# Gate and up blocks of a float32 decoder trunk: the closing adds and the silu issued later or as a side job, and the first block of a layer mixing single up chunks with its seven-product pairs

## The chip, the core and the metric

The kernel runs on one core of a Trainium2 chip. The metric is the device time of one execution in microseconds (us). TensorE is called PE here, VectorE DVE, ScalarE ACT, GpSimd POOL and the queue that issues the weight DMAs SP. All engines work their own instruction stream in order and wait for each other through semaphores.

## The reference

Two decoder layers on 256 tokens of width 2048. Each layer has a mixing part (attention, a linear recurrence and gated linear attention that share one input and one output projection) and a dense SwiGLU part. The change concerns the second:

```python
h = rms_norm(x, pre_ffn_norm[l])
hid = jax.nn.silu(einsum('bsd,df->bsf', h, w_ffn_gate[l])) * einsum('bsd,df->bsf', h, w_ffn_up[l])
ff = einsum('bsf,fd->bsd', hid, w_ffn_down[l])
x = x + rms_norm(ff, post_ffn_norm[l])
```

D is 2048 and the hidden width F is 5632. Everything is float32.

## The kernel before

**Matrix products.** Every float32 operand is split in two parts, hi (rounded to the fast matmul type) and lo (the rest), and one product is three matmuls: hi·hi, hi·lo, lo·hi (`multiply`, L393). The activations are split once. Each 128x512 chunk of weights is an *item* that must be split just before it is used: ACT copies it to hi, DVE subtracts to get lo (`split`, L301). The parts live in a ring of `NHI = 10` buffers called `hilo`, so that item n can be split only when the matmuls of item n-10 have read their buffer. Raw weights come in pieces of two chunks (512 KB) into a ring of `NRAW = 5` buffers; a piece is loaded when a slot is free (`load`, L279).

**Gate and up.** The hidden width is cut into 11 blocks of 512 (`f`), for two halves of the tokens (t = 0, 1). A block has eight pairs of chunks (`PAIRS = "CCCSCSCS"`). A C pair is done in the classic way: four items, each multiplied for both token halves (two products an item). An S pair is done with seven products in place of eight, in the manner of Strassen; its seven items are four sums of chunks made on DVE (t1 to t4) and three raw chunks. The products of an S pair are p1, p6, p7, q4, p2, q3, q5 in this order (`seven`, L435). p2, q4, q3 and x are four accumulators of the pool `acc`, used by C pairs as well; p1 sits in the PSUM tile `tr`, q5 in `o`, p6 and p7 are the two halves of the tile `sc`. So a block is 20 raw items with 40 products and 21 items with one product each: 61 products, 183 matmuls.

**The end of a block.** At the last S pair, after each product, `evac` (L1274) combines the sums: m1 is a copy of p1 (ACT); u2 = m1 + p6, u3 = u2 + p7, c21 = u3 + q4, c11 = m1 + p2, c12 = q3 - u2, c22 = x - u3 (DVE); silu of c21 and c11 (ACT); c12 and c22 get q5 added; each is scaled and multiplied with its silu (two scalar_tensor_tensor on DVE). In the profile u2 and u3 are named `u_u`, the four others `c_c`, m1 `m`. A side job, `hidden` (L1310), then transposes the result on PE into `tr` (t = 0) and `o` (t = 1), from where ACT and DVE write the split activations `uh` and `ul`. The next block's p1 and q5 use `tr` and `o` again, and `seven` demands that the job has been issued before it issues p1 (`lane.require`).

**What sets the order.** All is issued from one Python program that writes each engine's stream in the order of its calls. `feed(upto, used)` (L330) writes splits ahead: `LOOK_W = 12` items, as far as the ring lets it. At the last S pair of a block it is held back: after the seven products it may reach 0, 0, 1, 1, 2, 3 and 4 items past the block's end, and elsewhere in the block not past the end at all. Side jobs are run by `lane.tick()` when a modelled clock says that they are ready.

**The first block of a layer** (f = 0) multiplies the five classic pairs chunk by chunk: first ten gate chunks while the normalised input is still arriving, then `make_forms` (L1248, the sums of activations that the S pairs need: on DVE one add of 128x1536, four of 128x384, and three splits that ACT and DVE share), then ten up chunks, then three S pairs in a row.

After each part of four, four and three blocks come four `down` blocks over the finished hidden activations.

Of the kernel before, what the change touches and what calls it, by code (L numbers as in the profile page):

```python
# [15 lines left out]
AF = mybir.ActivationFunctionType  # L16
# [26 lines left out]


PAIRS = "CCCSCSCS"
FIRST_PAIRS = "CCCCCSSS"
N_C = PAIRS.count("C")
N_S = PAIRS.count("S")

# [1 line left out]
def pair_order(f):  # L51


    if f == 0:
        order = [(m, k) for m in range(2) for k in range(2 * N_C)]
        return order + [e for p in range(N_C, DC // 2) for e in quad(p)]
    order, at = [], {"C": 0, "S": N_C}
    for kind in PAIRS:
        p = at[kind]
        at[kind] += 1  # L60
        order += quad(p) if kind == "S" else [(m, k) for m in range(2) for k in (2 * p, 2 * p + 1)]
    return order
# [115 lines left out]
def tile_hybrid_trunk(ctx, tc, x, xT, w_in, w_out, w_gu, w_down, post_norms, lams,  # L178
# [74 lines left out]
    for l in range(DEPTH):  # L253
        for n0, n in IN_ORDER:
            plain(w_in[l][:, n0:n0 + n], DC)
        cols = [slice(b * 512, (b + 1) * 512) for b in range(4)]
        for c in cols:
            plain(w_out[l][:, c], DC)
        for f0, f1 in FFN_PARTS:
            for f in range(f0, f1):  # L260
                recipes = []
                for kind in FIRST_PAIRS if f == 0 else PAIRS:
                    i = sum(1 if r[0] == "raw" else 4 if r[0] == "b11" else 0 for r in recipes)
                    recipes += [("raw", i + j) for j in range(4)] if kind == "C" else [(name, i) for name in QUAD]
                add_block([w_gu[l, f, i] for i in range(DC)], recipes)
            for c in cols:
                plain(w_down[l][f0 * 512:f1 * 512, c], 4 * (f1 - f0))
# [3 lines left out]
    for b, (n, count) in enumerate(blocks):  # L271
        b %= per_layer
        w = b in (0, 14, 15, 16, per_layer - 2, per_layer - 1) and len(wider) > 0
        wider += [w and i % 8 in (1, 4, 6) and (b != 16 or i < 2 * N_C) for i in range(count)]
    raws, parts_of, rings = [], [], {False: [], True: []}
    before_load, before_split = {}, {}
    sums = {}
# [23 lines left out]
    def split():  # L301
        j = len(parts_of)
        b, kind, i = items[j]
        n = blocks[b][0]

        quad_of = {"b11": 1, "b21": 2, "b22": 3}
        r = raw_chunk(i + quad_of.get(kind, 0)) if kind == "raw" or kind in quad_of else sums[kind]
        before_split.pop(j, lambda: None)()
        if kind == "b11":
            up1, gate1, up2 = raw_chunk(i), raw_chunk(i + 1), raw_chunk(i + 3)  # L310
            dve.free = max(dve.free, raws[i // 2 + 1][1])
# [12 lines left out]
        dve.free = max(dve.free, act.free)  # L324
        dve.tensor_tensor(out=lo, in0=r, in1=hi.bitcast(F32), op=ALU.subtract)
        parts_of.append((hi, lo, dve.free))
        if (kind == "raw" and i % 2 or kind in ("t2", "b22")) and len(raws) < len(pieces):
            load()

    def feed(upto, used=math.inf):  # L330
# [71 lines left out]
    def pair_block(f, ah, al, forms, hidden_before, evac):  # L402
# [32 lines left out]
        def seven(j, p, final):  # L435
            if "p1" not in acc:
                lane.require(*hidden_before)
                acc["p1"] = pp.tile([P, 512], F32, tag="tr", name="gu_p1", bufs=1)
                acc["q5"] = pp.tile([P, 512], F32, tag="o", name="gu_q5", bufs=1)
                sc = pp.tile([P, 2, 512], F32, tag="sc", name="gu_p67", bufs=1)  # L440
                acc["p6"], acc["p7"] = sc[:, 0, :], sc[:, 1, :]
            s = [(forms[p][:, i, 0, :], forms[p][:, i, 1, :]) for i in range(4)]
            c = 2 * (N_C + p)
            a = {"p1": parted(c, 0), "p2": parted(c + 1, 0), "q4": parted(c + 1, 1),
                 "q5": s[0], "p6": s[1], "p7": s[2], "q3": s[3]}
            for i, k in enumerate(("p1", "p6", "p7", "q4", "p2", "q3", "q5")):
                feed(j + i + 1, used[0])
                multiply(acc[k], a[k], j + i, begin(k), final)
                used[0] = j + i + 1
                if final:  # L450
                    evac(k, acc)
                    feed(base + count + (0, 0, 1, 1, 2, 3, 4)[i], used[0])
                else:
                    feed(min(used[0] + LOOK_W, base + count), used[0])
                lane.tick()

        j = base
        if f == 0:
            at = [0, 0]
            while min(at) < 2 * N_C:  # L460
                able = [t for t in range(NT) if at[t] < 2 * N_C and (t == 1 or at[0] - at[1] < AHEAD)
                        and done.get(("h", t, at[t]), math.inf) <= lane.clk]
                if not able:
                    lane.idle()
                    continue
                t = min(able, key=lambda t: at[t])
                feed(j + at[t] + 1)
                classic(j + at[t], 0, at[t], t)
                at[t] += 1
                used[0] = j + min(at)  # L470
                if ("h", 1, 7) not in done:
                    feed(j + at[0] + LOOK_F, used[0])
                else:
                    feed(used[0] + LOOK_W, used[0])
            j += 2 * N_C
            forms.extend(make_forms(ah, al))
            for c in range(2 * N_C):
                feed(j + 1)
                for t in range(NT):
                    classic(j, 1, c, t)  # L480
                j += 1
                used[0] = j
                feed(min(j + LOOK_W, base + count), j)
            for p in range(N_S):
                seven(j, p, p == N_S - 1)
                j += 7
            return
        at = {"C": 0, "S": 0}
        for kind in PAIRS:
# [6 lines left out]
            for m in range(2):  # L496
                for c in (2 * p, 2 * p + 1):
                    feed(j + 1)
                    for t in range(NT):
                        classic(j, m, c, t)  # L500
                    j += 1
                    used[0] = j
                    feed(min(j + LOOK_W, base + count), j)


    def rsqrt(y, ss, n, inv, pre=None):
# [210 lines left out]
    for l in range(DEPTH):  # L717
# [551 lines left out]
        for part, (f0, f1) in enumerate(FFN_PARTS):  # L1269
            uh, ul = parts("uh"), parts("ul")  # L1270
            for f in range(f0, f1):
                got = {}

                def evac(k, acc, got=got, f=f, uh=uh, ul=ul):  # L1274
# [4 lines left out]
                    if k == "p1":  # L1279
# [3 lines left out]
                            pair = pm.tile([P, 2, 512], F32, tag="s4", name="_".join(names), bufs=NS4)  # L1283
                            got[names[0]], got[names[1]] = pair[:, 0, :], pair[:, 1, :]
                        act.copy(got["m1"], acc["p1"])
                    if k == "p6":
                        dve.free = max(dve.free, act.free)
                        add("u2", got["m1"], acc["p6"])
                    if k == "p7":
                        add("u3", got["u2"], acc["p7"])  # L1290
                        lane.free["sc"] = dve.free + W_DROP
                    if k == "q4":
# [3 lines left out]
                    if k == "q3":  # L1296
                        add("c12", acc["q3"], got["u2"], ALU.subtract)
                        add("c22", acc["x"], got["u3"], ALU.subtract)
                        for t, c in ((1, "c21"), (0, "c11")):
                            act.activation(got[c], got[c], AF.Silu, scale=s2f[t])  # L1300
                    if k == "q5":
                        for t, g, u in ((0, "c11", "c12"), (1, "c21", "c22")):
                            add(u, got[u], acc["q5"])
                        for t, g, u in ((0, "c11", "c12"), (1, "c21", "c22")):
                            dve.scalar_tensor_tensor(out=got[g], in0=got[u], scalar=s2f[t], in1=got[g],
                                                     op0=ALU.mult, op1=ALU.mult)
                        lane.free["tr"] = lane.free["o"] = dve.free + W_DROP
                        lane.add(0, hidden(f - f0, f, [got["c11"], got["c21"]], uh, ul))

                def hidden(c4, f, sg, uh, ul):  # L1310
                    for t in range(NT):
                        tag = "tr" if t == 0 else "o"
                        yield dve.through(0.25, tag) if t == 0 else (0.0, tag, None)
                        tp = turned(sg[t], tag, name="tpu")
                        split_scaled(uh[:, 4 * c4:4 * c4 + 4, t * P:(t + 1) * P],
                                     ul[:, 4 * c4:4 * c4 + 4, t * P:(t + 1) * P], tp, None)
                        dve.drops(tag)
# [30 lines left out]
W_SM = 0.25  # L1348
W_DROP = 0.3
W_AT = 0.1  # L1350


# [52 lines left out]
```

## Time and profile before

| what | us |
|---|---|
| median of 3 runs | 2290.61 (2290.44 to 2293.33) |
| the profiled execution, its own time | 2290.65 |
| its span, first to last instruction | 2288.8 |

| engine | busy us | share | instructions |
|---|---|---|---|
| PE weight loads | 1798.1 | 79% | 10206 |
| DVE | 1729.3 | 76% | 3175 |
| ACT | 1277.6 | 56% | 2561 |
| POOL | 13.3 | 1% | 33 |

The mean granted PE clock is 0.996. The weight DMAs move 409.75 MB in 512 KB pieces. Matmuls are pipelined: one is shown as 0.39 us long, but the next starts about 0.23 us after it. Time lost on PE is therefore best read from start to start, and idle time between the shown ends is somewhat less than what is lost. In the views a row has its start, its duration, engine, line, operation, output <- inputs, and in brackets the engine's idle time ahead of it with what ended it.

### The profile page before, as it was taken

Reading aid. Unit: us, or ns where it says so; the run is one execution under the profiler, and the core shown is the slowest. Engines: PE = TensorE matmul, PEld = TensorE weight load, DVE = VectorE, ACT = ScalarE, POOL = GpSimd, SP = SyncE. Lnnn points to the kernel's source line nnn. Section 1 sums busy time; section 2 is a strip of 40 time slices with the busy share of each in tenths; the row PEclk is TensorE's granted clock in tenths of the full one; section 3 lists DMA queues with packets and bytes.
Section 4 is the critical chain, followed back from the end, with each engine's and each line's share of the span. In section 5 each row is a group of like instructions: output and inputs, shape, how many; then the busy total and the mean of one; then the engine's idle time right before and its main releaser. Section 6 shows DMA issues by size and latency. Waiting matters only on the chain.

```text
span 2288.8 us, 30371 instructions
## 1 busy us (share of the span) xinstructions
PE 2217.9 (97%) x10206; PEld 1798.1 (79%) x10206; DVE 1729.3 (76%) x3175; ACT 1277.6 (56%) x2561; POOL 13.3 (1%) x33
## 2 busy tenths in 40 slices
PE   8999999899999999999999999998999999999998
PEld 7777878677787778877877788786777877788776
DVE  6766866898768886689786677569996588956885
ACT  6455755655545554455564467566555455544553
POOL 0000000000000000000000000000000000000000
PEclk9999999999999999999999999999999999999999
DMA  8553655365555546555654536544655555565464
GB/s 292 165 166 94 218 172 192 122 203 196 201 189 183 188 163 229 184 167 199 236 156 148 158 107 211 180 166 154 196 193 199 180 192 174 184 220 183 160 223 142
DMA packets 175068, 416.93 MB, mean 182 GB/s; under 512 B 13344, under 2 KB 24128, under 8 KB 174912
## 3 DMA queue, kind: packets, MB, share of 16 engines
q1 hardware_dynamic: 173056, 409.75, 54.3%
q0 software_dynamic: 1280, 4.20, 0.8%
q8 instruction: 80, 1.31, 0.2%
q10 hardware_dynamic: 576, 1.05, 0.1%
q14 instruction: 76, 0.62, 0.1%
HBM read 412.85 MB, written 2.10 MB: 181 GB/s over the span
## 4 chain that ended last, share of the span: by engine, by line
PE 85%; DVE 10%; issue 3%; ACT 1%; DMA 1%; SPq 0%; DVEq 0%; ACTq 0%
PE down L363 7%; PE in L362 7%; PE down L364 7%; PE down L362 6%; PE in L364 6%; PE in L363 6%; PE gu_q L398 5%; PE gu_q L399 5%; PE gu_q L397 5%; PE gu_p L397 4%; PE gu_p L399 4%; PE gu_p L398 4%; DVE hilo L158 4%; DVE c_c L158 3%; PE op L362 3%
## 5 line engine op out<-in xcount | busy, mean ns | idle before, releaser
L158 DVE TENSOR_TENSOR hilo<-raw,hilo 128x512 fp32r<-128x512 f32 (+1 forms) x1502 | 965.6, 675 | 343.9 <-ACT hilo L158 341.4
L158 ACT CAST hilo<-raw 128x512 fp32r<-128x512 f32 (+1 forms) x1502 | 857.7, 612 | 369.9 <-DVE hilo L158 183.6
L362 PE MATMUL in<-hilo,hh 128*128 128x512 f32 (+1 forms) x768 | 300.8, 392 | 6.1 <-ACT hilo L158 6.1
L364 PE MATMUL in<-hilo,hl 128*128 128x512 f32 (+1 forms) x768 | 287.4, 374 | 0.8 <-DVE hl L158 0.8
L363 PE MATMUL in<-hilo,hh 128*128 128x512 f32 (+1 forms) x768 | 286.7, 373 | 0.6 <-DVE hilo L158 0.6
L363 PE MATMUL down<-hilo,uh 128*128 128x512 f32 x704 | 274.5, 390 | 6.3 <-DVE hilo L158 6.3
L362 PE MATMUL down<-hilo,uh 128*128 128x512 f32 x704 | 274.6, 390 | 0.0
L364 PE MATMUL down<-hilo,ul 128*128 128x512 f32 x704 | 274.0, 389 | 0.0
L158 ACT CAST hilo<-t 128x512 fp32r<-128x512 f32 x264 | 162.4, 620 | 178.3 <-DVE t L158 141.9
L398 PE MATMUL gu_q<-hilo,hh 128*128 128x512 f32 x506 | 199.2, 394 | 15.4 <-DVE hilo L158 15.3
L397 PE MATMUL gu_q<-hilo,hh 128*128 128x512 f32 x506 | 197.9, 391 | 0.0
L399 PE MATMUL gu_q<-hilo,hl 128*128 128x512 f32 x506 | 197.7, 391 | 0.1
L158 DVE TENSOR_TENSOR hilo<-t,hilo 128x512 fp32r<-128x512 f32 x264 | 170.4, 684 | 4.4 <-ACT hilo L158 4.4
L362 PEld LDWEIGHTS in<-hilo,hh 128*128 128x128 f32 x768 | 145.2, 189 | 31.0 <-ACT hilo L158 6.5
L364 PEld LDWEIGHTS in<-hilo,hl 128*128 128x128 f32 x768 | 144.5, 188 | 27.5 <-DVE hl L158 1.3
L363 PEld LDWEIGHTS in<-hilo,hh 128*128 128x128 f32 x768 | 145.2, 189 | 22.4 <-DVE hilo L158 2.0
L363 PEld LDWEIGHTS down<-hilo,uh 128*128 128x128 f32 x704 | 132.2, 188 | 35.9 <-DVE hilo L158 8.8
L364 PEld LDWEIGHTS down<-hilo,ul 128*128 128x128 f32 x704 | 132.1, 188 | 27.3
L362 PEld LDWEIGHTS down<-hilo,uh 128*128 128x128 f32 x704 | 132.1, 188 | 27.1
L398 PE MATMUL gu_p<-hilo,hh 128*128 128x512 f32 x352 | 137.7, 391 | 2.3 <-DVE hilo L158 2.3
L397 PE MATMUL gu_p<-hilo,hh 128*128 128x512 f32 x352 | 137.8, 391 | 0.0
L399 PE MATMUL gu_p<-hilo,hl 128*128 128x512 f32 x352 | 137.3, 390 | 0.0
(221 smaller groups left out, 3116.0 us busy)
## 6 DMA issues: line engine op xcount, KB each, us to landing
raw<-in_w_gu_dram SPq DMA_DIRECT2D x352, 512.0 KB, 3.8
raw<-in_w_down_dram SPq DMA_DIRECT2D x176, 512.0 KB, 4.3
raw<-in_w_in_dram SPq DMA_DIRECT2D x159, 512.0 KB, 4.3
raw<-in_w_out_dram SPq DMA_DIRECT2D x64, 512.0 KB, 4.8
raw<-in_w_in_dram SPq DMA_DIRECT2D x32, 264.0 KB, 2.9
gain<-in_post_norms_dram POOLq DMA_DIRECT2D x16, 256.0 KB, 4.1
x<-in_x_dram SPq DMA_DIRECT2D x8, 256.0 KB, 7.5
xt<-in_xT_dram SPq DMA_DIRECT2D x7, 256.0 KB, 7.4
```

The lines of the kernel that those rows point to most:

```text
L158: return getattr(self.engine, name)(*args, **kwargs)
L362: nc.tensor.matmul(acc[t], ah[:, c, sl], hi, start=(i == 0), stop=False)
L363: nc.tensor.matmul(acc[t], ah[:, c, sl], lo, start=False, stop=False)
L364: nc.tensor.matmul(acc[t], al[:, c, sl], hi, start=False, stop=(i == last))
L397: nc.tensor.matmul(acc, a[0], hi, start=start, stop=False)
L398: nc.tensor.matmul(acc, a[0], lo, start=False, stop=False)
L399: nc.tensor.matmul(acc, a[1], hi, start=False, stop=stop)
```

## The change

It has four parts.

- **Order of the first block.** After the ten gate chunks the ten up chunks (U) and three S pairs are mixed: `UUUUUSUUUSUUS`. The weights are packed on the host in that order. A quad of an S pair can now lie across three pieces, so the loads follow a table, `read_by`, of pieces read to the end.
- **Look-ahead.** The limits at a block's end are gone: `feed` runs `LOOK_W` items ahead of the product just issued, across the end of the block, and at the last S pair before `evac` in place of after it.
- **u2 later.** u2 is issued after p7, with u3, in place of after p6.
- **Side job.** The two silu, the adds of q5, and the two scalar_tensor_tensor are steps of `hidden`, each at least `W_HID = 1` modelled us after the last, so that other work is written between them.

```diff
-FIRST_PAIRS = "CCCCCSSS"
+FIRST_ORDER = "UUUUUSUUUSUUS"
...
+    read_by, left = [], Counter()
+    for b, kind, i in items:
+        for c in {"raw": (i,), "b11": (i + 1,), "t2": (i,), "b21": (i + 2,), "b22": (i + 3,)}.get(kind, ()):
+            left[c // 2] += 1
+    full_at = 0
...
+        while full_at in left and left[full_at] == 0:
+            full_at += 1
+        read_by.append(full_at)
...
-        if (kind == "raw" and i % 2 or kind in ("t2", "b22")) and len(raws) < len(pieces):
+        while len(raws) < min(len(pieces), read_by[j] + NRAW):
             load()
...
                 multiply(acc[k], a[k], j + i, begin(k), final)
                 used[0] = j + i + 1
+                feed(used[0] + LOOK_W, used[0])
                 if final:
                     evac(k, acc)
-                    feed(base + count + (0, 0, 1, 1, 2, 3, 4)[i], used[0])
-                else:
-                    feed(min(used[0] + LOOK_W, base + count), used[0])
                 lane.tick()
...
             forms.extend(make_forms(ah, al))
-            for c in range(2 * N_C):
+            at = {"U": 0, "S": 0}
+            for kind in FIRST_ORDER:
+                p = at[kind]
+                at[kind] += 1
+                if kind == "S":
+                    seven(j, p, p == N_S - 1)
+                    j += 7
+                    continue
                 feed(j + 1)
                 for t in range(NT):
-                    classic(j, 1, c, t)
+                    classic(j, 1, p, t)
                 j += 1
                 used[0] = j
-                feed(min(j + LOOK_W, base + count), j)
-            for p in range(N_S):
-                seven(j, p, p == N_S - 1)
-                j += 7
+                feed(j + LOOK_W, j)
             return
...
-                    feed(min(j + LOOK_W, base + count), j)
+                    feed(j + LOOK_W, j)
...
-                    if k == "p6":
+                    if k == "p7":
                         dve.free = max(dve.free, act.free)
                         add("u2", got["m1"], acc["p6"])
-                    if k == "p7":
                         add("u3", got["u2"], acc["p7"])
                         lane.free["sc"] = dve.free + W_DROP
...
-                        for t, c in ((1, "c21"), (0, "c11")):
-                            act.activation(got[c], got[c], AF.Silu, scale=s2f[t])
                     if k == "q5":
-                        for t, g, u in ((0, "c11", "c12"), (1, "c21", "c22")):
-                            add(u, got[u], acc["q5"])
-                        for t, g, u in ((0, "c11", "c12"), (1, "c21", "c22")):
-                            dve.scalar_tensor_tensor(out=got[g], in0=got[u], scalar=s2f[t], in1=got[g],
...
+                        lane.add(0, hidden(f - f0, f, got, acc["q5"], uh, ul))
+
+                def hidden(c4, f, got, q5, uh, ul):
+                    names = ("c11", "c12"), ("c21", "c22")
+                    yield after(W_HID)
+                    for t, (g, u) in enumerate(names):
+                        act.activation(got[g], got[g], AF.Silu, scale=s2f[t])
+                        dve.tensor_tensor(out=got[u], in0=got[u], in1=q5, op=ALU.add)
+                        yield after(W_HID)
+                    lane.free["tr"] = lane.free["o"] = dve.free + W_DROP
+                    for t, (g, u) in enumerate(names):
+                        dve.free = max(dve.free, act.free)
+                        dve.scalar_tensor_tensor(out=got[g], in0=got[u], scalar=s2f[t], in1=got[g],
+                                                 op0=ALU.mult, op1=ALU.mult)
+                        yield after(W_HID)
                     for t in range(NT):
...
-                        tp = turned(sg[t], tag, name="tpu")
+                        tp = turned(got[names[t][0]], tag, name="tpu")
...
+W_HID = 1.0
```

The changed kernel has the same instructions on every engine, kind by kind; only their order differs. Three places show how.

**DVE at the end of block 1** (layer 0; the same at the end of every gate and up block). `hilo<-raw` are subtractions for the next block's first items. Before:

```order
L158 TENSOR_TENSOR hilo<-t_4650,hilo 128x512
L158 TENSOR_TENSOR u_u_4726<-m_4725,gu_p_4544 128x512
L158 TENSOR_TENSOR u_u_4726<-u_u_4726,gu_p_4544 128x512
L158 TENSOR_TENSOR hilo<-raw,hilo 128x512
L158 TENSOR_TENSOR c_c_4727<-u_u_4726,gu_q_4377 128x512
L158 TENSOR_TENSOR c_c_4727<-m_4725,gu_p_4376 128x512
```

Now:

```order
L162 TENSOR_TENSOR hilo<-t_4650,hilo 128x512
L162 TENSOR_TENSOR hilo<-raw,hilo 128x512 x6
L162 TENSOR_TENSOR u_u_4742<-m_4741,gu_p_4544 128x512
L162 TENSOR_TENSOR u_u_4742<-u_u_4742,gu_p_4544 128x512
L162 TENSOR_TENSOR hilo<-raw,hilo 128x512
L162 TENSOR_TENSOR c_c_4743<-u_u_4742,gu_q_4395 128x512
L162 TENSOR_TENSOR hilo<-raw,hilo 128x512
L162 TENSOR_TENSOR c_c_4743<-m_4741,gu_p_4394 128x512
```

Ahead of c21 (the first `c_c`) stand seven subtractions of the next block where one stood, ahead of c11 (the second) eight.

**PE around the transposes `tpu` of block 0's result** (layer 0), which lie inside block 1. Before, they stand in that block's fourth item, 51 matmuls ahead of its first p1:

```order
L399 MATMUL gu_q_4378<-hilo,hl 128x512
L551 MATMUL tpu<-ident,c_c_4327 128x128 x8
L397 MATMUL gu_x<-hilo,hh 128x512
L398 MATMUL gu_x<-hilo,hh 128x512
L399 MATMUL gu_x<-hilo,hl 128x512
L397 MATMUL gu_p_4376<-hilo,hh 128x512
```

Now they stand behind all twelve items of the first three C pairs. The first row behind them is p1 (`gu_p_4542`), which goes into the PSUM tile that the transposes of t = 0 have just filled:

```order
L417 MATMUL gu_x<-hilo,hl 128x512
L571 MATMUL tpu<-ident,c_c_4343 128x128 x8
L415 MATMUL gu_p_4542<-hilo,hh 128x512
L416 MATMUL gu_p_4542<-hilo,hh 128x512
L417 MATMUL gu_p_4542<-hilo,hl 128x512
L415 MATMUL gu_p_4544<-hilo,form 128x512
```

The job's steps take their distance, and the demand at p1 issues the rest of it at once. Counted in matmuls between the transposes and p1, this place reads 0 for blocks 0, 1 and 2, 9 for block 4, 6 for block 5, 3 for block 6, 9 for block 8 and 6 for block 9, in both layers. Behind blocks 3, 7 and 10 come `down` blocks, with no p1 near.

**DVE in the first block around `make_forms`** (the rows `mw` and `form`; layer 0). `hl` is the last of the normalised input. Before:

```order
L158 TENSOR_TENSOR hilo<-raw,hilo 128x512 x2
L158 SCALAR_TENSOR_TENSOR hl<-tpx,vec,hh 128x128 x4
L158 TENSOR_TENSOR hilo<-raw,hilo 128x512 x4
L158 TENSOR_TENSOR mw<-hh,hl 128x1536
L158 TENSOR_TENSOR mw<-mw 128x3x128 x4
L158 TENSOR_TENSOR form<-mw,form 128x4x128 x3
```

Now:

```order
L162 TENSOR_TENSOR hilo<-raw,hilo 128x512
L162 TENSOR_TENSOR t_4016<-raw 128x512
L162 TENSOR_TENSOR t_4018<-t_4016,raw 128x512
L162 TENSOR_TENSOR hilo<-raw,hilo 128x512
L162 SCALAR_TENSOR_TENSOR hl<-tpx,vec,hh 128x128 x4
L162 TENSOR_TENSOR t_4043<-raw 128x512
L162 TENSOR_TENSOR t_4045<-t_4018,raw 128x512
L162 TENSOR_TENSOR hilo<-t_4018,hilo 128x512
L162 TENSOR_TENSOR hilo<-t_4043,hilo 128x512
L162 TENSOR_TENSOR hilo<-t_4045,hilo 128x512
L162 TENSOR_TENSOR hilo<-raw,hilo 128x512
L162 TENSOR_TENSOR mw<-hh,hl 128x1536
```

The first S pair's sums and five of its splits have come ahead of `make_forms`, in place of five up chunks' splits; the first product that needs a form stood behind ten up chunks and now stands behind five.

More of the change, by code (lines that the diff above doesn't have):

```diff
@@ L54, in pair_order @@
     if f == 0:
-        order = [(m, k) for m in range(2) for k in range(2 * N_C)]
-        return order + [e for p in range(N_C, DC // 2) for e in quad(p)]
+        order, at = [(0, k) for k in range(2 * N_C)], {"U": 0, "S": N_C}
+        for kind in FIRST_ORDER:
+            order += quad(at[kind]) if kind == "S" else [(1, at[kind])]
+            at[kind] += 1
+        return order
     order, at = [], {"C": 0, "S": N_C}
@@ L261, in tile_hybrid_trunk @@
                 recipes = []
-                for kind in FIRST_PAIRS if f == 0 else PAIRS:
-                    i = sum(1 if r[0] == "raw" else 4 if r[0] == "b11" else 0 for r in recipes)
-                    recipes += [("raw", i + j) for j in range(4)] if kind == "C" else [(name, i) for name in QUAD]
+                i = 0
+                for kind in "G" * 2 * N_C + FIRST_ORDER if f == 0 else PAIRS:
+                    k = 1 if kind in "GU" else 4
+                    recipes += [(name, i) for name in QUAD] if kind == "S" else [("raw", i + j) for j in range(k)]
+                    i += k
                 add_block([w_gu[l, f, i] for i in range(DC)], recipes)
@@ L274, in tile_hybrid_trunk @@
         wider += [w and i % 8 in (1, 4, 6) and (b != 16 or i < 2 * N_C) for i in range(count)]
+    read_by, left = [], Counter()
[3 more added lines that the diff above has]
+    full_at = 0
+    for b, kind, i in items:
+        for c in {"raw": (i,), "b11": (i + 1,), "t2": (i,), "b21": (i + 2,), "b22": (i + 3,)}.get(kind, ()):
+            left[c // 2] -= 1
+        while full_at in left and left[full_at] == 0:
+            full_at += 1
+        read_by.append(full_at)
     raws, parts_of, rings = [], [], {False: [], True: []}
@@ L310, in split @@
             up1, gate1, up2 = raw_chunk(i), raw_chunk(i + 1), raw_chunk(i + 3)
-            dve.free = max(dve.free, raws[i // 2 + 1][1])
+            dve.free = max(dve.free, raws[(i + 3) // 2][1])
             summed("t1", gate1, up1, "e")
@@ L476, in pair_block @@
             forms.extend(make_forms(ah, al))
-            for c in range(2 * N_C):
+            at = {"U": 0, "S": 0}
+            for kind in FIRST_ORDER:
+                p = at[kind]
+                at[kind] += 1
+                if kind == "S":
+                    seven(j, p, p == N_S - 1)
+                    j += 7
+                    continue
                 feed(j + 1)
                 for t in range(NT):
-                    classic(j, 1, c, t)
+                    classic(j, 1, p, t)
                 j += 1
                 used[0] = j
-                feed(min(j + LOOK_W, base + count), j)
-            for p in range(N_S):
-                seven(j, p, p == N_S - 1)
-                j += 7
+                feed(j + LOOK_W, j)
             return
@@ L1298, in evac @@
                         add("c22", acc["x"], got["u3"], ALU.subtract)
-                        for t, c in ((1, "c21"), (0, "c11")):
-                            act.activation(got[c], got[c], AF.Silu, scale=s2f[t])
                     if k == "q5":
-                        for t, g, u in ((0, "c11", "c12"), (1, "c21", "c22")):
-                            add(u, got[u], acc["q5"])
-                        for t, g, u in ((0, "c11", "c12"), (1, "c21", "c22")):
-                            dve.scalar_tensor_tensor(out=got[g], in0=got[u], scalar=s2f[t], in1=got[g],
[L1306 to L1310, printed above, removed]
+                        lane.add(0, hidden(f - f0, f, got, acc["q5"], uh, ul))
[12 more added lines that the diff above has]
+                        yield after(W_HID)
                     for t in range(NT):
```

## The prediction

> **What bounds the kernel now.** The page comes first: PE is busy nearly all the time, so only PE's gaps can be won. The list of waits (who waited for whom: us in total, times, longest) says which of them lie in the gate and up blocks.
>
> ```profile
> PE 2217.9 (97%) x10206; PEld 1798.1 (79%) x10206; DVE 1729.3 (76%) x3175; ACT 1277.6 (56%) x2561; POOL 13.3 (1%) x33
> ```
> ```profile
> PE gu_p L397 <- DVE u_u L158: 22.8, 22, 2.9
> PE gu_q L398 <- DVE hilo L158: 15.3, 15, 1.1
> PE gu_p L398 <- DVE hilo L158: 9.0, 10, 1.7
> PE down L363 <- DVE hilo L158: 6.3, 6, 1.1
> ```
>
> Together 53.4 us: most of what PE stands idle. The 22 waits for `u_u` are one per block, the 21 of the second and fourth row come behind a block's end, and the ten of the third belong to the two first blocks. The timeline of PE shows the first two kinds in one block (block 2, layer 0), from p1 of its last S pair on:
>
> ```profile
> 534.51 0.39 PE L397 MATMUL gu_p<-hilo,hh 128*128 128x512 f32 x1
> ...
> 535.19 0.39 PE L397 MATMUL gu_p<-hilo,form 128*128 128x512 f32 x1
> ...
> 535.64 0.39 PE L399 MATMUL gu_p<-hilo,form 128*128 128x512 f32 x1
> 536.88 0.50 PE L397 MATMUL gu_p<-hilo,form 128*128 128x512 f32 x1 [0.85 <-DVE u_u L158]
> 537.22 0.40 PE L398 MATMUL gu_p<-hilo,form 128*128 128x512 f32 x1
> ...
> 540.44 0.39 PE L397 MATMUL gu_p<-hilo,hh 128*128 128x512 f32 x1
> ...
> 544.52 0.39 PE L397 MATMUL gu_q<-hilo,hh 128*128 128x512 f32 x1
> 545.95 0.50 PE L398 MATMUL gu_q<-hilo,hh 128*128 128x512 f32 x1 [1.04 <-DVE hilo L158]
> ...
> 546.52 1.03 PE L551 MATMUL tpu<-ident,c_c 128*128 128x128 f32 x8
> 547.31 0.47 PE L397 MATMUL gu_x<-hilo,hh 128*128 128x512 f32 x1
> ```
>
> A product takes 0.68 (534.51 to 535.19), its three matmuls 0.227 each. p7 starts at 536.88, 1.24 behind the matmul before it: 1.01 lost, and 0.11 in the step after it (0.34). At 545.95 it is 1.43: 1.20 lost, and 0.11 again. So **a block's end costs 2.43 us**; the next block starts at 540.44. DVE and ACT there:
>
> ```profile
> 538.49 0.69 DVE L158 TENSOR_TENSOR hilo<-raw,hilo 128x512 fp32r<-128x512 f32 x1
> 539.09 0.68 DVE L158 TENSOR_TENSOR c_c<-u_u,gu_q 128x512 f32<-128x512 f32 x1
> 539.69 0.68 DVE L158 TENSOR_TENSOR c_c<-m,gu_p 128x512 f32<-128x512 f32 x1
> ```
> ```profile
> 535.39 0.59 ACT L158 COPY m<-gu_p 128x512 f32<-128x512 f32 x1 [3.37 <-PE gu_p L399]
> 535.87 1.14 ACT L158 CAST hilo<-raw 128x512 fp32r<-128x512 f32 x2
> ```
>
> DVE starts an operation every 0.60 (538.49, 539.09, 539.69), ACT one every 0.5, each in the order written. c21 and c11 (the two `c_c`) end at 539.77 and 540.37, just before 540.44. That matters, because the next block's first two accumulators are the buffers that c21 and c11 have read: q4's buffer, free first, is given out first, p2's second.
>
> **The end of a block after the change.** The wait for u2 and the wait for the fourth item's split both go: u2 and u3 follow p7, and ten splits are written ahead. What is late next is c21 and c11, now behind seven and eight subtractions of the next block (41 is its first item). I walk the queues with p1's start as 0. A product has left its buffers some 0.9 after its start (m's copy of p1 starts at 535.39, p1 at 534.51), so the ring buffer of product i (0 for p1) is free at 0.68 i + 0.90. Item 44 takes p1's buffer: cast 0.90 to 1.5. Then ACT copies m1, casts item 45 at 1.9, and item 46, which needs p7's buffer (2.26), at 2.45 to 3.05. DVE subtracts 44 at 1.55, 45 at 2.6, 46 at 3.2; u2 starts at 3.8; u3, which reads it, at 4.5; a subtraction at 5.1; **c21 from 5.7 to 6.4**; a subtraction at 6.3; **c11 from 6.9 to 7.6**. PE ends the seven products at 4.76 and gets its first buffer at 6.4; three matmuls later, at about 7.2, it needs the second and gets it at 7.65, where 5.44 was due. With 0.11 for starting again 2.3 us are lost in place of 2.43. **Twenty ends (blocks 1 to 10, both layers): -2.6 us**, out of the 48.6 that were there. The adds of q5, the silu and the two last multiplications come behind these and release nothing that PE wants soon; put back ahead of c11 each would cost 0.60 on DVE.
>
> The loads don't reach this path: the last piece that the walk uses is asked for when its ring slot's last subtraction ends, about 1.8 ahead of p1, is cast at 4.3, and lands in 3.8 (first row below).
>
> ```profile
> raw<-in_w_gu_dram SPq DMA_DIRECT2D x352, 512.0 KB, 3.8
> L158 ACT CAST uh<-tpu x44: 576/586/594, 460.1 to 2222.2; 128x512 fp32r<-128x512 f32 x44
> L158 DVE TENSOR_TENSOR ul<-tpu,uh x44: 677/682/686, 463.5 to 2223.4; 128x512 fp32r<-128x512 f32 x44
> ```
>
> **A new wait: p1 behind the transposes.** Where p1 follows the transposes directly, it waits until ACT (0.59) and DVE (0.68) have read `tr`, and all of PE is queued behind it. Before shows no such wait. Bounds: nothing, if both ran beneath the eight transposes (0.79, 546.52 to 547.31); about 2 us, if both began only when all eight are done, with one cast ahead of them. Walked with the transposes' start as 0: the product before them starts at -0.68, its ring buffer is cast from 0.22 to 0.84, `uh` runs from 0.75 to 1.35; DVE subtracts that item at 0.88 and makes `ul` from 1.48 to 2.16; p1 starts at 2.2, due at 0.79. With the restart 1.5 us; I take it, nearer the upper end, since the ring puts that cast and subtraction ahead. Six places: 9 us. With three matmuls between (block 6) 0.68 more is hidden and one cast less stands ahead: 0.6, twice. With six or nine there is no wait. **Together +10.2 us.**
>
> **The first block.** DVE sets the pace here, and its work is the same in a new order.
>
> ```profile
> 421.29 1.90 DVE L158 TENSOR_TENSOR form<-mw,form 128x512 fp32r<-128x512 f32 x3 [0.69 <-ACT form L158]
> 423.10 0.15 DVE L158 TENSOR_REDUCE ss<-ssx 128x2 f32<-128x8 f32 x1
> ...
> 449.94 0.69 DVE L158 TENSOR_TENSOR c_c<-m,gu_p 128x512 f32<-128x512 f32 x1
> ```
> ```profile
> 446.26 0.79 PE L397 MATMUL gu_p<-hilo,form 128*128 128x512 f32 x1 [2.87 <-DVE u_u L158]
> ...
> 451.12 0.39 PE L397 MATMUL gu_p<-hilo,hh 128*128 128x512 f32 x1
> 456.20 0.50 PE L398 MATMUL gu_q<-hilo,hh 128*128 128x512 f32 x1 [0.62 <-DVE hilo L158]
> ```
>
> Before, block 1 starts at 451.12 and loses 0.9 at 456.20 (0.62 idle, the rest as above): as if it started at 452.0. After, six operations stand between the last `hl` and `make_forms` where four stood, two of them sums that casts wait for: the forms start 0 to 3.6 later (six operations at 0.60), I take 2.05, so at 423.35. From there to c11's end the new order has the three forms (1.8), 13 small operations of the norm (0.15 each, 2.2 with their gaps), and 41 operations of 0.60 with 0.4 for sums that read the one before: 29.0, so c11 ends at 452.4, and block 1 starts as if at 451.9. **Nothing won**: what PE no longer waits inside the block it waits at its end, 5 us in one piece. Such a piece makes the clock slow:
>
> ```profile
> 442.28:445.69 3.41, 0.73 (x2) 0.30 (x2) 3.41 (x7) 3.41 (x7) 0.00 (x0) 1.00 0.46 154
> 445.69:449.10 3.41, 2.84 (x7) 2.26 (x8) 1.67 (x3) 1.40 (x2) 0.00 (x0) 0.50 0.47 154
> ...
> 1148.84:1152.25 3.41, 2.12 (x11) 1.45 (x12) 3.41 (x9) 2.83 (x11) 0.00 (x0) 1.00 0.14 25
> ```
>
> (stretch, length, busy us of PE, PEld, DVE, ACT and POOL, granted clock, DMA). A stretch of 3.41 us with 0.73 of PE work was followed by one at 0.50, one with 2.12 was not. Before paid such a stretch already, inside the wait of 446.26; after pays it behind the block's start, up to 1.7 each. **+2 us for both layers** (0 to 3.4).
>
> **Sum**, against the profiled execution's own time: 2290.65 - 2.6 + 10.2 + 2 = 2300.3 us; its 1.85 outside the span stay. It lies within 0.1 us of the median of the runs (2290.61).
>
> **Rivals.**
> - *The clock falls at ordinary ends too.* After the change PE idles 1.5 and 0.25 (between shown ends) within 2.7 us: a stretch that holds it all has 1.65 of work, between the 0.73 that slowed and the 2.12 that did not. If half of the 22 ends fall on the bad side, 11 x 1.6 = +17.6: 2318. The Trainium skill, "TensorE: Matmul & The Clock Gate", Part 1, says that the clock halves after at least one idle window of about 3.4 us; by that no ordinary end would slow and the time would be 2300. The trace speaks against taking it to the letter: 0.73 us of work stood in the stretch ahead of 445.69.
> - *p1's wait is hidden* since ACT and DVE reach the transposed tile at once: 2290.65 - 2.6 + 2 = 2290, the same. It needs `ul` done 0.8 after the transposes' start; 0.59 and 0.68 in a row alone are more.
> - *Faster: the ends really close.* If c21 starts by 4.0 and c11 by 4.65 behind p1, PE finds both buffers free, and the ends lose nothing: 2290.65 - 48.6 + 10.2 + 2 = 2254. It needs all six subtractions done when u2 can start at 2.3, so the casts of items 44 to 46 before p1, p6 and p7 release their buffers: against the ring. For it: ACT stood idle 3.37 ahead of m.
> - *The first blocks gain* what PE lost inside them (9.0 and 2 x 2.87 of idle time, some 18 with restarts), if DVE's order frees c11 sooner: 2282. That the mixing brings nothing there is part of my forecast.
>
> **How the numbers follow.** Forecast 0.62 (its own range 2293 to 2308); slower clock 0.15; p1's wait hidden 0.13; ends close 0.06; first blocks gain 0.04. The range 2286 to 2318 leaves out the two faster cases and half of the slow-clock case. 0.2%, or 4.6 us, is what a measurement of this kernel can tell from no change: faster has the two faster cases and a sliver, 0.11; within it lie most of the hidden-p1 case and the forecast's low end, 0.18; slower keeps 0.71.
>
> **What would show it.** In the list of waits PE's waits for `u_u` are gone, as are those for `hilo` at block starts; in their place stand waits for `c_c`, two at each of 22 block ends, near 1.5 and 0.25, and eight waits of p1 for `ul`, six near 1.2. On DVE's timeline c21 starts 5.7 behind p1. The stretch from one block's last p7 to the next one's, 44.9 now, is 46.3 where p1 follows the transposes directly and 44.7 elsewhere. I am wrong if c21 starts before 4.5, if p1 waits under 0.7, or if the clock row shows 0.50 behind most ends.

## The result, and the profile after

| | median us | runs | profiled execution | its span | mean granted PE clock |
|---|---|---|---|---|---|
| before | 2290.57 | 2290.44 to 2293.33 | 2290.65 | 2288.8 | 0.996 |
| after | 2315.87 | 2312.89 to 2316.99 | 2312.89 | 2310.8 | 0.989 |

The changed kernel is slower: the ratio is 1.0106, 95% interval 1.0088 to 1.0123. The profiled execution was the fastest of its four, 3 us below their median. All sums below are made against it.

The first line of the page, with the engines' busy time, has the same counts as before. PE was busy 2217.9 before:

```profile
PE 2233.3 (97%) x10206; PEld 1809.9 (78%) x10206; DVE 1743.9 (75%) x3175; ACT 1303.8 (56%) x2561; POOL 13.3 (1%) x33
```

The same 10206 matmuls are shown busy 15.4 us longer. That is the first sign of a slower clock, since a busy time does not contain waits. The list of waits on PE (who waited for whom: us in total, times, longest):

```profile
PE gu_p L415 <- DVE c_c L162: 32.7, 16, 5.1
PE down L380 <- DVE c_c L162: 10.8, 12, 1.6
PE gu_p L415 <- DVE ul L162: 7.8, 8, 1.2
PE gu_p L415 <- ACT form L162: 6.3, 2, 3.2
...
PE gu_q L415 <- DVE c_c L162: 2.4, 14, 0.2
...
PE down L380 <- ACT uh L162: 0.8, 2, 0.4
```

The waits for `u_u` and, at block starts, for `hilo` are gone. In their place every block end waits for c21 and c11 (`c_c`), eight p1 wait for `ul`, and each first block waits once for a form. PE's timeline at the end of block 2 (layer 0), the place that the prediction showed of before; p1 of the last S pair starts at 538.53:

```profile
538.53 0.39 PE L415 MATMUL gu_p<-hilo,hh 128*128 128x512 f32 x1
...
543.06 0.39 PE L417 MATMUL gu_q<-hilo,form 128*128 128x512 f32 x1
545.08 0.47 PE L415 MATMUL gu_p<-hilo,hh 128*128 128x512 f32 x1 [1.63 <-DVE c_c L162]
545.39 0.40 PE L416 MATMUL gu_p<-hilo,hh 128*128 128x512 f32 x1
545.63 0.39 PE L417 MATMUL gu_p<-hilo,hl 128*128 128x512 f32 x1
546.19 0.50 PE L415 MATMUL gu_q<-hilo,hh 128*128 128x512 f32 x1 [0.17 <-DVE c_c L162]
546.53 0.40 PE L416 MATMUL gu_q<-hilo,hh 128*128 128x512 f32 x1
```

The four starts behind 543.06, 545.08, 545.63 and 546.19 come 2.02, 0.31, 0.56 and 0.34 later where 0.227 is normal: 2.32 lost (the second step stands between 545.08 and 545.39). The seven products themselves run without a gap. DVE there:

```profile
541.73 0.69 DVE L162 TENSOR_TENSOR hilo<-raw,hilo 128x512 fp32r<-128x512 f32 x1
542.33 0.68 DVE L162 TENSOR_TENSOR u_u<-m,gu_p 128x512 f32<-128x512 f32 x1
543.05 0.69 DVE L162 TENSOR_TENSOR u_u<-u_u,gu_p 128x512 f32<-128x512 f32 x1
543.66 0.68 DVE L162 TENSOR_TENSOR hilo<-raw,hilo 128x512 fp32r<-128x512 f32 x1
544.26 0.68 DVE L162 TENSOR_TENSOR c_c<-u_u,gu_q 128x512 f32<-128x512 f32 x1
544.86 0.68 DVE L162 TENSOR_TENSOR hilo<-raw,hilo 128x512 fp32r<-128x512 f32 x1
545.46 0.68 DVE L162 TENSOR_TENSOR c_c<-m,gu_p 128x512 f32<-128x512 f32 x1
```

c21 starts 5.73 behind p1 and ends at 544.94; PE starts at 545.08. c11 ends at 546.14; PE takes the second buffer at 546.19.

**Where the 22 us went.** For each matmul of the gate, up and down blocks and each first matmul behind transposes I took the distance to the start before it, less 0.227, and sorted the sums by what the matmul waited for; matmuls without a wait that lie in a stretch of half clock are the last row but one.

| lost on PE, us | before | after | difference | forecast |
|---|---|---|---|---|
| ends of 20 ordinary blocks | 44.4 | 42.9 | -1.5 | -2.6 |
| the two first blocks and their ends | 17.8 | 16.6 | -1.2 | 0 |
| p1 behind the transposes | 0 | 8.4 | +8.4 | +10.2 |
| `down` behind the transposes | 0 | 1.4 | +1.4 | none |
| slow clock, both first blocks | 3.9 | 8.9 | +5.0 | +2 |
| slow clock, ordinary ends | 0 | 10.0 | +10.0 | 0 |
| the rest | 3.2 | 3.4 | +0.2 | none |
| sum | 69.3 | 91.6 | +22.3 | +9.6 |

The spans differ by 22.0, so the table is complete. The ends' row after comes to 2.13 at 19 of the 20 ends; one, at 1696.42, waited 0.28 longer. The other 0.19 of the 2.32 lies in matmuls that show no wait (545.39 and 546.53) and stands in the rest.

The slow clock is seen in the view by stretches (stretch, length, busy us of PE, PEld, DVE, ACT and POOL, granted clock, DMA share, GB/s). Two ordinary ends of the changed kernel, each with the stretch behind it:

```profile
1741.82:1745.23 3.41, 1.68 (x7) 0.77 (x5) 3.38 (x7) 1.29 (x3) 0.00 (x0) 1.00 0.80 282
1745.23:1748.65 3.42, 3.35 (x8) 2.68 (x9) 3.42 (x7) 1.97 (x3) 0.00 (x0) 0.50 0.48 160
588.12:591.53 3.41, 1.78 (x9) 1.19 (x8) 3.38 (x6) 2.14 (x4) 0.00 (x0) 1.00 0.73 226
591.53:594.95 3.42, 3.25 (x14) 2.33 (x14) 3.42 (x7) 2.03 (x4) 0.00 (x0) 1.00 0.71 253
```

At the first, 1.68 us of PE work in a stretch of 3.41 were followed by a stretch at 0.50; at the second 1.78 were not. Both hold the whole long piece of 1.63 (it ends at 1744.19 and at 591.34); the first has 0.1 of the short piece as well. So between these two it is the sum of idle time in the stretch that differs, not the longest piece. The stretches lie on a grid of their own (the slow ones that begin at 724.66, 861.19 and 994.31 are 40 and 39 times 3.413 apart), so the ends of different blocks are cut by it in different places. Six of the 20 ordinary ends were slowed, at 1.60 to 1.71 us each: the 10.0 us of the table.

### The profile page after: what moved, and what is told of

The parts are those of the page before. It is cut to its first block, busy times and chain, and to the rows that moved or that the text cites. A ratio compares the mean times of both kernels' runs of the same rounds, so it can differ in the third digit from the quotient of the medians.

```text
span 2310.8 us, 30317 instructions
## 1 busy us (share of the span) xinstructions
PE 2233.3 (97%) x10206; PEld 1809.9 (78%) x10206; DVE 1743.9 (75%) x3175; ACT 1303.8 (56%) x2561; POOL 13.3 (1%) x33
## 4 chain that ended last, share of the span: by engine, by line
PE 85%; DVE 8%; issue 2%; ACT 2%; DMA 1%; SPq 0%; ACTq 0%; DVEq 0%
PE down L380 7%; PE down L382 7%; PE down L381 7%; PE in L380 6%; PE in L382 6%; PE in L381 6%; PE gu_q L415 5%; PE gu_q L417 5%; PE gu_q L416 5%; DVE hilo L162 4%; PE gu_p L415 4%; PE gu_p L416 4%; PE gu_p L417 4%; PE op L380 3%; PE op L382 3%; PE op L381 3%
## 5 line engine op out<-in xcount | busy, mean ns | idle before, releaser
L162 DVE TENSOR_TENSOR hilo<-raw,hilo 128x512 fp32r<-128x512 f32 (+1 forms) x1502 | 984.2, 676 | 420.9 <-ACT hilo L162 415.1
L162 ACT CAST hilo<-raw 128x512 fp32r<-128x512 f32 (+1 forms) x1502 | 877.8, 613 | 438.1 <-DVE hilo L162 166.3
L415 PE MATMUL gu_q<-hilo,hh 128*128 128x512 f32 x506 | 201.9, 399 | 2.4 <-DVE c_c L162 2.4
L416 PE MATMUL gu_q<-hilo,hh 128*128 128x512 f32 x506 | 199.9, 395 | 0.0
L415 PE MATMUL gu_p<-hilo,hh 128*128 128x512 f32 x352 | 142.1, 404 | 40.5 <-DVE c_c L162 32.7
L416 PE MATMUL gu_p<-hilo,hh 128*128 128x512 f32 x352 | 139.5, 396 | 0.0
```

The costliest lines, as they stand in the source:

```text
L162: return getattr(self.engine, name)(*args, **kwargs)
L415: nc.tensor.matmul(acc, a[0], hi, start=start, stop=False)
L416: nc.tensor.matmul(acc, a[0], lo, start=False, stop=False)
```

## The experiments

Each ran beside the kernel before on the same chip, whose medians there were 2291.03 (the first four), 2290.56 (the next four) and 2290.93 (the last two). Lost times are sums as in the table above, of the profiled execution.

**1. One subtraction fewer ahead of c21 and c11.** In `seven`, `evac` is put back ahead of `feed`:

```diff
-                feed(used[0] + LOOK_W, used[0])
                 if final:
                     evac(k, acc)
+                feed(used[0] + LOOK_W, used[0])
```

> One edit to the changed kernel: at the last S pair evac is called ahead of feed, so one subtraction fewer stands on DVE ahead of u2, c21 and c11 (five, six and seven in place of six, seven and eight). Theory A (the clock is slowed by the idle time at block ends, and only when it passes some 1.7 us in a stretch of 3.41): an end costs 1.7 in place of 2.3, 22 x 0.6 = -13, and the slow stretches behind blocks 1 to 10 vanish, some 7 x 1.6 = -11: about 2292. Rival B (the slow stretches come from something else, the transposes or the loads): only -13, 2303, and the slow stretches stay.

Measured: 2290.19 (2289.19 to 2292.68), ratio 0.9998 (0.9989 to 1.0007), as theory A had it. The stretches of its ends that hold least PE work:

```profile
1724.75:1728.16 3.41, 2.18 (x9) 1.19 (x9) 3.41 (x7) 1.83 (x3) 0.00 (x0) 1.00 0.65 222
1728.16:1731.57 3.41, 3.41 (x16) 2.81 (x15) 3.41 (x6) 2.21 (x5) 0.00 (x0) 1.00 0.60 210
```

Waits for `c_c` sum 40.5 in place of 52.9, slow clock 7.0 in place of 18.8, none of it at an ordinary end. One operation of 0.60 on DVE cost 12.4 us as waits (0.56 at each of 22 ends), and as much again because it took the ends to where the clock falls: the profiled times differ by 23.7.

**2. The side job earlier.** In the classic loop of an ordinary block, ahead of the third C pair:

```diff
+            if p == 2:
+                lane.require(*hidden_before)
             for m in range(2):
```

> One edit to the changed kernel: the side job is demanded ahead of the third C pair, so the transposes stand 24 matmuls ahead of p1 in every block. Theory A: PE's waits for ul ahead of p1 vanish (8 waits, 8.4 us with restarts in the profile), -8 to -10: about 2307, with the waits for c_c at block ends as they were. Rival: the wait only moves to the transposes, since the last two multiplications on DVE are not done by then: 2316.

Measured: 2296.45 (2293.93 to 2299.74), ratio 1.0022 (1.0011 to 1.0032). The transposes now stand 24 matmuls ahead of p1 and no p1 waits for `ul`. The profiled executions differ by 13.2: 8.4 of these waits and 4.6 of slow clock. The medians differ by 19.4, more than was expected. The profiled execution was the slowest of its eight, at a mean clock of 0.991, where five of the others had 0.994; 0.003 of 2297 is 7 us of granted clock, so most executions had less slow clock than the one with the trace. In which stretches can't be read. The waits for `c_c` stayed (53.2 against 52.9), so the two losses are separate.

**3. The first block in its old order.**

```diff
-FIRST_ORDER = "UUUUUSUUUSUUS"
+FIRST_ORDER = "UUUUUUUUUUSSS"
```

> One edit to the changed kernel: the order of the first block is as before (ten up chunks, then three S pairs). Theory A (DVE paces the first block, so the order is worth nothing): the 3.1 us wait of p6 for the forms goes, waits inside the S pairs come back, and c11 of that block ends within 1 us of where it ended (452.4 in layer 0): 2314 to 2318. Rival: the mixing costs what its new wait for the forms shows, twice 3.3: 2309. Rival: the mixing gains, and without it the time goes to 2325.

Measured: 2317.14 (2312.81 to 2317.24), ratio 1.0109 (1.0093 to 1.0124): no difference from the changed kernel, as theory A had it. The wait for the form is gone and ten waits for splits are back, the same ten as before the change:

```profile
PE gu_p L416 <- DVE hilo L162: 9.0, 10, 1.7
```

**4. The look-ahead held at three items.** At the last S pair:

```diff
-                feed(used[0] + LOOK_W, used[0])
+                feed(min(used[0] + LOOK_W, base + count + 3) if final
+                     else used[0] + LOOK_W, used[0])
```

> One edit to the changed kernel: at the last S pair the look-ahead stops three items past the block's end, so no subtraction stands between m1 and c22. Theory A (what is left at a block's end is only DVE's queue ahead of c21 and c11): c21 ends 4.3 and c11 4.9 after p1's start, both before PE wants their buffers (4.76 and 5.44), so the ends cost under 0.3: -2.2 x 22 = -48; the slow stretches behind ends go, -11; the waits of p1 stay at about 7 in all: 2250 to 2262. Rival C: the look-ahead is needed there, and PE waits for the fourth item's split as before, 1.3 an end: 2280.

Measured: 2255.32 (2251.70 to 2257.31), ratio 0.9841 (0.9825 to 0.9857). DVE's timeline at the end of block 1, layer 0:

```profile
489.00 0.69 DVE L162 TENSOR_TENSOR hilo<-raw,hilo 128x512 fp32r<-128x512 f32 x1 [0.66 <-ACT hilo L162]
490.41 0.69 DVE L162 TENSOR_TENSOR u_u<-m,gu_p 128x512 f32<-128x512 f32 x1 [0.72 <-PE gu_p L417]
491.14 0.69 DVE L162 TENSOR_TENSOR u_u<-u_u,gu_p 128x512 f32<-128x512 f32 x1
491.93 0.69 DVE L162 TENSOR_TENSOR c_c<-u_u,gu_q 128x512 f32<-128x512 f32 x1
492.53 0.68 DVE L162 TENSOR_TENSOR c_c<-m,gu_p 128x512 f32<-128x512 f32 x1
```

u2 now waits 0.72 for p7 where it stood behind a queue, and c21 and c11 follow with nothing between. The 20 ordinary ends lose nothing that shows as a wait; the two first blocks still wait 2.9 each. Slow clock falls to 5.0 and waits for `ul` rise to 13.1. So the wait at the ends, the slow clock behind it and 58 us in all come from the items of look-ahead past the third.

**5. Both: held at three, the job earlier.**

> Edit: at the last S pair of a block the look-ahead is held to three adds of the next block (as e4), and the side job with the hidden operands' transposes is called for ahead of the third C pair (as e2). Theory A (the two losses of the changed kernel are independent: 2.3 us at each block end from the adds of the next block ahead of the closing adds, and waits of p1 for the last transposes): e4 took 2255.3 with 13.1 us of waits of gu_p for ul; these go, so 2242 (2239 to 2246). Rival B (the transposes' wait only moves to another matmul, since VectorE is behind there whatever the place): 2255 again, with the same 13 us at another tile.

Measured: 2244.36 (2242.37 to 2247.41), ratio 0.9798 (0.9784 to 0.9813). No p1 waits for `ul`. Theory A holds.

**6. As 5, with the first block in its old order.**

> Edit: as e5, and the first block of a layer in its old order (ten U, then three S). Theory A (VectorE paces the first block whatever the order, so mixing is worth nothing there): within 3 us of e5, the first block's losses moved from the wait for forms to the hilo reads. Rival B (mixing is worth something once nothing else is lost at the block ends): 5 to 12 us slower than e5.

Measured: 2243.44 (2243.36 to 2245.14), ratio 0.9795 (0.9780 to 0.9809). It can't be told from 5: the mixing is worth nothing here either. This is the fastest of all, with 5 beside it.

**7. The same stall in one piece.** c21 goes next to c11:

```diff
-                    if k == "q4":
-                        add("c21", got["u3"], acc["q4"])
                     if k == "p2":
+                        add("c21", got["u3"], acc["q4"])
```

> Edit: the changed kernel with c21 issued next to c11, two adds later, so that the stall of TensorE at a block end comes in one piece in place of two and is no longer in sum. Theory A (the slow clock is set by how much TensorE works within one stretch of 3.41 us; 1.62 us was too little and 1.78 enough): the same 2.3 us lost per end, but slow stretches after more than half of the 22 ends in place of about 6, 1.7 us each: 2326 (2318 to 2336). Rival B (the slow stretches do not come from the ends' idle time): as many as in the changed kernel, 2316.

Measured: 2326.90 (2322.78 to 2328.51), ratio 1.0152 (1.0135 to 1.0168). PE at the end of block 2, and a stretch of such an end with the one behind it:

```profile
547.96 0.60 PE L415 MATMUL gu_p<-hilo,hh 128*128 128x512 f32 x1 [2.23 <-DVE c_c L162]
```
```profile
1882.74:1886.15 3.41, 1.35 (x6) 0.77 (x5) 3.38 (x7) 1.90 (x4) 0.00 (x0) 1.00 0.80 282
1886.15:1889.57 3.42, 3.25 (x8) 2.61 (x9) 3.42 (x7) 0.99 (x2) 0.00 (x0) 0.50 0.48 164
```

As theory A had it, more than half of the ordinary ends were slowed: 13 in place of 6. Slow clock cost 30.5 in place of 18.8. The stall was not quite the same: the waits for `c_c` sum 59.3, 6.4 more than in the changed kernel. Of the 15.4 by which the profiled times differ the slow clock has most.

**8. The old limits of the look-ahead.** The changed kernel, with nothing fed past a block's end but at its last products:

```diff
                 if final:
                     evac(k, acc)
+                    feed(base + count + (0, 0, 1, 1, 2, 3, 4)[i], used[0])
+                else:
+                    feed(min(used[0] + LOOK_W, base + count), used[0])
...
-                feed(j + LOOK_W, j)
+                feed(min(j + LOOK_W, base + count), j)
```

> Edit: the changed kernel with the old limits of the look-ahead (no adds of the next block ahead of the end of this one); u2 later, the side job and the first block's order stay. Theory A (the look-ahead over the end is the one part that spoils the change; with c21, u2 and c11 right behind the last pair's adds they are done before the next block's third pair reads their banks): the ends close, about 2255 with waits for ul as in e4 (13 us), and faster than before by 1.5 per cent. Rival B (a block that begins without adds made ahead stalls on its own first pairs, 1.2 to 1.3 us an end): 2280 to 2290.

Measured: 2293.84 (2287.45 to 2295.59), ratio 1.0009 (1.0000 to 1.0019). Neither theory. The ends nearly close, as A had it (9.3 lost for `c_c`: 3.2 at the two first blocks and 0.3 at each ordinary end, too short for the list of waits), and the fourth item did not wait. But the transposes stand three matmuls ahead of all 16 p1, and each loses some 2.06 where such a place lost 0.85 to 0.91 in most blocks of experiment 4:

```profile
PE gu_p L415 <- DVE ul L162: 30.3, 16, 2.0
```

33.0 us are lost there, and 15.9 to ten slow stretches. Why the wait is so much longer than in experiment 4 isn't shown.

**9. The old limits, the job earlier.** 8 and 2 together.

> Edit: the changed kernel with the old limits of the look-ahead (as in e8), and the side job called for ahead of the third C pair (as in e2). e8 lost 33 us in sixteen waits of p1 for ul and some 16 us to slow stretches, and nothing at the block ends. Theory A (those waits come from the place of the transposes, and the slow stretches from the waits): both go, 2250 (2244 to 2258), so the look-ahead across the end is worth nothing even where it does no harm. Rival B (without adds made ahead a block's first items run late wherever the job stands): waits of the same sum at other tiles, 2275 or more.

Measured: 2270.51 (2269.81 to 2270.80), ratio 0.9910 (0.9896 to 0.9925). The waits of p1 and most of the slow clock went (4.6 us of 15.9 are left), but the transposes themselves now wait for the last multiplication (`c_c` here):

```profile
PE tpu L575 <- DVE c_c L162: 19.0, 16, 1.2
```

This is rival B's mechanism at a price between the two. Experiment 5 differs from it in the limits of the look-ahead alone (at the last S pair three items past the end at once, against 0, 0, 1, 1, 2, 3 and 4 after the seven products), and is 26.1 us faster: look-ahead across the end is worth something, as long as it stops before it delays c21 and c11.

**10. u2 later, alone, in the kernel before.** DVE's order stays; p7 need not wait until u2 has read p6 in the other half of `sc`.

```diff
-                    if k == "p6":
+                    if k == "p7":
                         dve.free = max(dve.free, act.free)
                         add("u2", got["m1"], acc["p6"])
-                    if k == "p7":
                         add("u3", got["u2"], acc["p7"])
```

> Edit: the kernel before with one part of the change alone: the sum u2 is issued after p7, with u3, in place of after p6. VectorE's order stays the same, only p7 no longer waits until u2 has read p6, which lies in the other half of the same tile. Theory A (p7's wait is all that this order cost): the 22 waits for u_u go, 26 us with what is lost at starting again: 2264 (2262 to 2270). Rival B (u2, u3, c21 and c11 come some 0.8 us later and the next block waits for their buffers): 0.5 us or more an end comes back, 2275 to 2285.

Measured: 2278.86 (2278.63 to 2279.35), ratio 0.9947 (0.9931 to 0.9964). This is in rival B's range. The 22 waits for `u_u` are gone (26.3 lost), and with them the slow clock of the first blocks (3.9). What comes back is of two kinds, about equal. One is at the buffers, as B had it: c21 now ends at 537.00, and the next block's first matmul, due 0.23 behind the one before, starts 0.53 behind it:

```profile
536.61 0.39 PE L399 MATMUL gu_q<-hilo,form 128*128 128x512 f32 x1
537.14 0.47 PE L397 MATMUL gu_p<-hilo,hh 128*128 128x512 f32 x1
```

With the step behind it this is 0.38 at each of the 20 ordinary ends, 7.7 in all, too short for the list of waits; the two first blocks lose another 3.3. The other, some 10, is at the fourth item's split, which stands behind the closing adds and multiplications on DVE, and which PE now reaches sooner:

```profile
PE gu_q L398 <- DVE hilo L158: 23.2, 16, 1.5
PE down L363 <- DVE hilo L158: 8.6, 6, 1.4
```

Before, these two groups showed 15.3 and 6.3. This part alone makes the kernel faster by 0.5%.

## Why the prediction was too low

The direction and most terms held; the size did not: +9.6 was forecast, +22.3 came in the profiled execution and +25.3 between the medians. By its own steps:

- **The end of a block, -2.6.** Right, by the walk itself: c21 5.7 behind p1 was 5.73, the first buffer at 6.4 came at 6.55, the second at 7.65 was used at 7.66, and 2.3 lost was 2.32. From 2.43 to 2.32 is 2.2 for twenty ends; the table's row shows 1.5, without the steps of starting again and with the one longer wait. Experiment 4 shows that the queue of subtractions ahead of c21 and c11 is the cause, and 1 that one of them, 0.60 on DVE, costs 0.56 an end.
- **p1 behind the transposes, +10.2.** Right in place, kind and count (eight, six of them long), 1.8 too high. The timeline of PE at block 1, layer 0:

```profile
469.46 1.03 PE L571 MATMUL tpu<-ident,c_c 128*128 128x128 f32 x8
471.70 0.50 PE L415 MATMUL gu_p<-hilo,hh 128*128 128x512 f32 x1 [1.21 <-DVE ul L162]
```

  1.2 idle was forecast, 1.21 was shown. Four short waits of `down` behind the transposes, 1.4 together, I had left out.
- **The first block, nothing won.** Nearly right: -1.2 in the table, and experiments 3 and 6 say the same from the other side. Block 1 was to start as if at 451.9, behind one piece of 5 us; it started at 451.29, behind one wait of 5.05.
- **The clock at the first blocks, +2.** Too low, at +5.0. I counted the piece at the end only; the wait for the form, 3.13 long, slows the clock a second time:

```profile
424.27:427.68 3.41, 3.41 (x9) 2.63 (x8) 3.06 (x15) 3.09 (x6) 0.00 (x0) 0.50 0.00 0
...
448.16:451.57 3.41, 0.28 (x1) 0.32 (x2) 3.38 (x6) 2.50 (x4) 0.00 (x0) 0.50 1.00 363
451.57:454.99 3.42, 3.42 (x9) 2.60 (x9) 3.42 (x7) 1.45 (x3) 0.00 (x0) 0.50 0.65 225
```

- **The clock at ordinary ends, 0.** This is the step that failed. The prediction had worked out that a stretch which holds a whole end has 1.65 us of PE work, between the 0.73 that was known to slow and the 2.12 that was known not to, and then put nothing for it in the sum and 0.15 on a rival with 17.6. The trace of before had closer bounds to offer, in layer 1: 1.42 was followed by 0.50, and 1.79 was not (two pairs below). They too leave 1.65 open, but give no ground for a term of nothing. The runs put the border at 1.6 to 1.8, right on the 1.65, so that about a third of the ends fall on the bad side: +10.0 in the profile. Experiment 1 moves the ends to 2.18 and above and none is slowed; 7 moves them down and 13 are. The rule that I had weighed there, the Trainium skill's "TensorE: Matmul & The Clock Gate", Part 1, by which it takes at least one idle window of about 3.4 us, does not hold here to the letter: 1.68 us of work stood in the window ahead of 1745.23. Its window of 3413 ns that runs free of the kernel does agree with the stretches of 3.41 and their grid.

```profile
1565.26:1568.67 3.41, 1.79 (x8) 1.42 (x9) 3.41 (x8) 2.96 (x6) 0.00 (x0) 1.00 0.45 154
1568.67:1572.08 3.41, 2.82 (x13) 2.02 (x12) 3.38 (x7) 0.96 (x2) 0.00 (x0) 1.00 0.47 153
...
1578.92:1582.33 3.41, 1.42 (x5) 0.51 (x4) 3.41 (x7) 3.03 (x6) 0.00 (x0) 1.00 0.47 159
1582.33:1585.74 3.41, 1.68 (x4) 1.39 (x5) 1.67 (x3) 2.56 (x4) 0.00 (x0) 0.50 0.44 153
```

The profiled difference of 22.3 exceeds the forecast of 9.6 by 12.7. The two terms of the clock are too low by 13.0 together; the others miss by -1.8 (p1), +1.4 (`down`), +1.1 (ends), -1.2 (first blocks) and +0.2 (the rest), and that these nearly cancel is luck. Where the 3 us from the profiled execution to the median come from isn't shown: two more slow stretches at 1.65 would do it, but the mean clocks of the four executions (0.989, and 0.988 to 0.990 in the others) don't bear that out.

What the change was meant to win is there all the same. p7's wait for u2 and the fourth item's wait, 44.4 us in the 20 ends, both went. The look-ahead of up to ten items, where three do no harm, put nearly the same time back as a wait for c21 and c11, and the side job's late place put 8.4 on top. Without those two the same change takes 2244 (experiment 5).

## What to carry to other kernels

Work written ahead on an engine that runs in order stands ahead of the operations that free PSUM, and each piece costs TensorE nearly its full length once the queue has no slack (0.56 of 0.60 us in experiment 1): cap the look-ahead at what fits before these operations are due, rather than remove the cap or the look-ahead. Place a side job's transposes by when both their inputs are ready and their reader's buffer is wanted, and move them with the look-ahead. When a change leaves idle pieces of a microsecond or two on TensorE, reckon how much work remains in the worst stretch of 3.41 us that holds them, and where it comes near half a stretch, put the slow clock into the sum and not among the rivals.

## What was not expected of the hardware

- **The border of the clock.** A full-speed stretch with up to 1.68 us of PE work in the changed kernel was followed by one at 0.50, one with 1.78 and above was not. Over all runs the border is blurred, perhaps because matmul ends are modelled: in experiment 2 a stretch with 1.78 was followed by 0.50, in 7 two with 1.65 and 1.69 and in 8 one with 1.63 were not. It lies near half of the stretch, far from an idle one.
- **The price of a slow stretch.** Each cost 1.60 to 1.71 us where PE had work throughout, half its length. Where it lay inside a wait, as from 448.16 to 451.57 with 0.28 of work, it cost next to nothing.
- **Spread from run to run.** Kernels whose waits lie near the border spread more: 8.1 us over ten runs of experiment 8, and 5.8 over eight of experiment 2, against 0.7 over the four of experiment 10, which had no slow stretch but at its end. In 2, 4 and 5 the slowest execution had the lowest mean clock and the fastest the highest (in 4, 0.995 at 2257.31 and 0.998 at 2251.70). That the grid falls differently in each execution would explain it; with one trace a kernel this is not shown.
